# Four edits to a tuned encoder layer: a scale moved forward, a split between two prompt products, weight loads cut into eight pieces, and the down projection begun with another product

## The chip, the core and the metric

The kernel runs on one core of one Trainium2 chip. The time is device microseconds (us) of one execution on that core; the median of three executions is what counts. Five instruction queues run beside each other and wait for one another by semaphores: TensorE (PE, with its weight loads listed apart as PEld), VectorE (DVE), ScalarE (ACT), GpSimd (POOL), and SyncE (SP), which here only issues DMAs.

## The reference, cut to what matters

```python
h = _rmsnorm(x, g_mix)
z = h @ w_in
# qa, ka, va, qb, kb, vb and gates are slices of z
o_a, _ = _banded_attention(qa, ka, va, A_WINDOW, 1, rel_bias[:, :A_HEADS], sink)
o_b = _dilated_mixture(qb, kb, vb, rel_bias[:, A_HEADS:])
merged = gates[:, :, 0] * (o_a.reshape(b, S, A_Q) @ w_branch_a) + gates[:, :, 1] * (o_b @ w_branch_b)
x = x + merged @ w_out
h = _rmsnorm(x, g_mlp)
return x + jnp.square(jax.nn.relu(h @ w_up)) @ w_down
```

One layer of this is run, with a last RMSNorm behind it, over 1024 "sample" rows and 256 "prompt" rows of width 1024; the hidden width is 4096. Everything is float32.

## The kernel before, in words

A float32 product is made of three products of rounded parts. Each operand is split into a high part (ACT copies it rounded, the name ends in `hi`) and a low part (DVE subtracts the high one, the name ends in `lo`), and `six` multiplies low by high, high by low and high by high. For the sample rows the seven products of a Strassen-Winograd scheme (A11, A12, S2, S3, S1, A22, S4) stand for eight: sums and differences of weight quarters (`ta`, `tb`) and of activation quarters are split and multiplied. The prompt rows go through plain products (`prompt`). Every engine's queue runs in the order in which the program is written; there is no planner. Generators (`turns`, `b`/`nb`, `hooks`, `side`) are advanced at written places to put one stage's instructions among another's.

The stages in order are these. RMSNorm of ten tiles of 128 rows: `square(t)` and `scale(t)` on ACT and DVE, then `turn` transposes the tile on PE (names `tr`), beside the first value products (L794, `v`). Then pairs of 128-column blocks of `w_in`: `pair` runs the seven products of one pair while `right_pair` loads, combines and splits the weights of the next (`raw`, `ta`, `tb`, `whi`, `wlo`). The last five pairs are "late": between their products attention B runs, a step at each `beside()`; each step needs its `qk` and `v` loads, which SP issues (L509, L512, L524). Then attention A, the branch products and `w_out`. Then sixteen calls `up(j)` for the up projection: seven sample products and two prompt products each, with the split of the next weights between them, squared ReLU on ACT and DVE (L1869 to L1874), and on POOL four combinations of the result (L1945 to L1948) that are stored to `scr_u` by seven DMAs. `up(0)` has its two prompt products at its end, and the first two products of `up(1)` are computed before them.

The down projection is 28 jobs `(n, g)`: product n of seven, for the eight hidden blocks of group g. The first fourteen jobs take groups 0 and 1, two jobs to a product, and accumulate in the same PSUM banks. A job is 60 matmuls of 128x512 (`dn`). While job s runs, `ahead(s)` issues the `fetch` of the left side of job s+2 from `scr_u` (`uraw`, three DMAs), weight blocks (`loads`) and residual rows (`residual`, five DMAs to `v`), splits the weights of job s+1 (`dhi`, `dlo`; from a loaded block, or from a difference `t` of two that POOL makes in `combine`, L1698), and splits the left side of job s+1 (`uhi`, `ulo`, `up`; `left`, three parts, each after one of the job's five tiles). After a pair of jobs DVE adds each tile to the residual sums (L1852). `begin` does the same for job 0 and part of job 1 during the last `up`, one step at each hook.

`up(15)` is the last of these calls. The instructions of interest are, by the names of the profile: `xn<-xt,rs,gm` and `tr<-ident,xn` in the first stage, `raw<-in_w_in_dram` and `qk<-scr_qb` in the late pairs, `whi<-ta`, `wlo<-ta`, `wlo<-tb` in `up(0)` and `up(1)`, and `dhi`, `ulo`, `t` and `v<-scr_x` around the first jobs of the down projection.

Of the kernel before, what the change touches and what calls it, by code (L numbers as in the profile page):

```python
# [10 lines left out]
F32 = mybir.dt.float32  # L11
# [4 lines left out]
P = 128  # L16
# [81 lines left out]
def encoder_kernel(  # L98
# [224 lines left out]
    def steps_of(gen, n):  # L323
        for _ in range(n):
            next(gen, None)
# [43 lines left out]

    def right_pair(cols, out, make=wslot, vector=False):  # L370

# [4 lines left out]
        for i in range(2):  # L376
            nc.sync.dma_start(raw[i], cols[i])
        yield

# [289 lines left out]
    with ExitStack() as pre:  # L669
# [173 lines left out]
        scale(2)  # L843
        next(turns[0], None)
        pss = [bank("mm", "v") for _ in range(2)]
        for t, i in ((0, 0), (0, 1), (1, 0), (1, 1), (0, 2), (1, 2), (0, 3), (1, 3)):
# [3 lines left out]
        next(turns[2])  # L850
        square(3)
        next(turns[1], None)
        scale(3)
        square(4)
# [53 lines left out]
    if True:  # L908
# [104 lines left out]
        def pair(b, parts, cols, nxt, hooks, beside, late):  # L1013
# [5 lines left out]
            np_ = []  # L1019
            nb = right_pair([w_in3[:, :, c : c + P] for c in nxt], np_, wslot, late) if nxt else iter(())  # L1020

# [5 lines left out]
            def behind():  # L1027
                beside()
                if not late:
                    steps_of(b, 2)  # L1030

            one.begin()
# [10 lines left out]
            next(hooks, None)  # L1043
            one.direct(NS, NP, pa)
            beside()
            seven(x, S2, parts[1], 0, False, False, beside)
            c2 = stage("c", n=2)
            nc.scalar.activation(c2, x, AF.Copy, scale=one.scale)
            behind()
            if late:  # L1050
                next(nb, None)
            z = bank("mm", "z")
            seven(z, S3, parts[1], 1, last=False, mid=beside)
            c7 = stage("c", n=2)
            nc.scalar.activation(c7, z, AF.Copy, scale=two.scale)
            two.begin()
            beside()
            next(hooks, None)
            seven(x, S1, parts[2], 0, False, False, beside)
            two.sum(512, 512, x, c7)  # L1060
            beside()
            if not late:
                steps_of(nb, 3)
# [592 lines left out]
    TO = ((C22, C12), (C11,), (C12,), (C21, C22), (C12,), (C21,), (C11,))  # L1656
    JOBS = [(n, 2 * p + i) for p in range(NG // 2) for n in range(7) for i in range(2)]

    class Down:
# [6 lines left out]

        def block(self, g, k, h, make=wslot, queue=None):

            b = self.blocks[g, k, h] = [make("raw", (P, 2, 512)) for _ in range(2)]
            for i in range(2):  # L1670
                j = 4 * g + 2 * i
                (queue or nc.sync).dma_start(b[i], w_down4[:, j : j + 2, k, 512 * h : 512 * h + 512])

        def loads(self, n, g):
            if n == 1:
                self.block(g, 1, 1, slot)
            elif n == 4:
                self.block(g, 1, 0, slot)
            elif n == 5 and g < NG - 2:
                self.block(g + 2, 0, 0)  # L1680
                self.block(g + 2, 0, 1)

# [70 lines left out]
        def begin(self):  # L1753

            self.block(0, 0, 0, wslot, nc.scalar)
            self.block(0, 0, 1, slot, nc.scalar)
            self.fetch(*JOBS[0])
            yield
            self.combine(*JOBS[0])
            yield  # L1760
            yield
            self.block(1, 0, 0)
            self.block(1, 0, 1)
            yield
            self.right(*JOBS[0], slot)
            self.combine(*JOBS[1])
            yield
            self.left(*JOBS[0], 0)
            self.left(*JOBS[0], 1)
            yield  # L1770
            self.fetch(*JOBS[1])
            yield
            self.left(*JOBS[0], 2)

        def ahead(self, s):
# [86 lines left out]
    with ExitStack() as pre:  # L1862
# [22 lines left out]

        begun = {}

        def up(j, b, parts, hooks):
# [6 lines left out]

            u = [stage(f"u{i}", TH) for i in range(7)]
            u11, u12, u22, u21 = u[A11], u[A12], u[A22], u[S3]
            start = begin(parts)
# [4 lines left out]
            steps_of(b, 2)  # L1903
            next(hooks, None)
            x, y, c1 = begun[j] if j in begun else next(start)
            relu2_sum(u11[:, :512], y, c1)
# [40 lines left out]
            nc.gpsimd.tensor_tensor(u[S3], u11, u21, op=ALU.subtract)  # L1947
            nc.gpsimd.tensor_tensor(u[S4], u12, u[S2], op=ALU.subtract)  # L1948
            for i in (A11, S1, A22, S2, S3, A12, S4):
                nc.sync.dma_start(scr_u[j // 4][:, i, j % 4, :], u[i])  # L1950
            next(hooks, None)
# [48 lines left out]
```

## Time and profile before

| | |
|---|---|
| median of 3 runs | 1686.62 us (1685.78 to 1687.19) |
| profiled execution, its own time | 1685.92 us |
| its span | 1684.1 us, granted clock 0.999 |
| PE busy | 1667.8 us (99%) |
| DVE, ACT, POOL busy | 952.2, 718.3, 511.6 us |
| DMA | 260.35 MB, mean 155 GB/s |

A row of a timeline begins with the start in us from the span's beginning and the length in us; the bracket at its end is the time for which the engine stood idle before it, and what ended that. Matmuls overlap in the pipeline: two that follow each other without a gap start 0.23 us apart though each is shown 0.39 us long. A row with xN stands for N instructions in a row. A row of the waits gives engine, line, what was waited for, total us, times, longest us. A row of windows gives, for a stretch, its length, the busy time of each engine and at its end granted clock, DMA share and GB/s.

### The profile page before, as it was taken

The numbers are of one execution on the slowest core, as the hardware profiler recorded it, in microseconds if no ns is written. First come the engines' busy times: TensorE is split into PE (matmuls) and PEld (weight loads), VectorE is DVE, ScalarE is ACT, GpSimd is POOL, SyncE is SP. The second block draws the span as 40 slices with busy tenths as digits, with TensorE's granted clock in tenths as the row PEclk, the third lists the DMA queues.
The fourth block names the chain that finished last, engine by engine and source line by source line (L and its number), as shares of the span: only waits on it lengthen the run. The fifth ranks groups of instructions, "written<-read, shape, count | busy, mean of one in ns | idle before, by whom it ended". The sixth has DMA issues, their size and how long they took to land.

```text
span 1684.1 us, 24915 instructions
## 1 busy us (share of the span) xinstructions
PE 1667.8 (99%) x9268; PEld 1413.9 (84%) x9268; DVE 952.2 (57%) x1544; ACT 718.3 (43%) x1485; POOL 511.6 (30%) x404
## 2 busy tenths in 40 slices
PE   8999999999999999999999999999999999999998
PEld 7898888887788888888888888888888888888886
DVE  6732233455563565677278445545457767666575
ACT  6332323346663556654175333333334333333345
POOL 1312222122111463200100646556456322314150
PEclk9999999999999999999999999999999999999999
DMA  7416552677676793845121443443346845533333
GB/s 247 150 58 127 134 129 77 163 193 196 191 198 189 202 244 118 293 130 198 38 88 58 160 152 111 136 160 119 121 160 241 293 155 166 207 101 114 119 119 125
DMA packets 224408, 260.35 MB, mean 155 GB/s; under 512 B 29568, under 2 KB 154288, under 8 KB 224288
## 3 DMA queue, kind: packets, MB, share of 16 engines
q1 hardware_dynamic: 214976, 235.60, 44.1%
q0 software_dynamic: 7936, 20.54, 5.5%
q10 hardware_dynamic: 1376, 2.62, 0.4%
q8 instruction: 73, 1.20, 0.3%
q14 instruction: 47, 0.39, 0.1%
HBM read 173.03 MB, written 90.92 MB: 157 GB/s over the span
## 4 chain that ended last, share of the span: by engine, by line
PE 92%; DVE 3%; ACT 2%; DMA 1%; issue 1%; SPq 1%; POOL 0%; DVEq 0%; ACTq 0%
PE dn L347 20%; PE x L347 19%; PE mm L192 14%; PE z L347 9%; PE v L794 5%; PE mm L347 5%; PE y L347 5%; PE sc L347 3%; PE pv L347 3%; PE pv L1173 1%; PE pt L1157 1%; PE sc L537 1%; PE pv L582 1%; PE pt L569 1%; PE sc L1131 1%
## 5 line engine op out<-in xcount | busy, mean ns | idle before, releaser
L347 PE MATMUL dn<-dhi,ulo 128*128 128x512 f32 x448 | 174.5, 390 | 2.0 <-DVE ulo L186 2.0
L347 PE MATMUL dn<-dlo,uhi 128*128 128x512 f32 x448 | 174.3, 389 | 0.0
L347 PE MATMUL dn<-dhi,uhi 128*128 128x512 f32 x448 | 174.3, 389 | 0.0
L347 PE MATMUL x<-chi,wlo 128*128 128x512 f32 x424 | 167.2, 394 | 1.7 <-DVE wlo L314 1.6
L347 PE MATMUL x<-clo,whi 128*128 128x512 f32 x424 | 165.7, 391 | 0.1
L347 PE MATMUL x<-chi,whi 128*128 128x512 f32 x424 | 165.1, 389 | 0.0
L314 DVE TENSOR_TENSOR wlo<-ta,whi 128x1024 fp32r<-128x1024 f32 x30 | 55.7, 1857 | 178.5 <-ACT whi L312 178.5
L314 DVE TENSOR_TENSOR wlo<-raw,whi 128x1024 fp32r<-128x1024 f32 x60 | 90.4, 1506 | 97.8 <-ACT whi L312 97.8
L389 POOL TENSOR_TENSOR tb<-raw 128x512 f32<-128x512 f32 x25 | 32.8, 1312 | 364.4 <-DMA raw<-in_w_in_dram 147.0
L347 PEld LDWEIGHTS dn<-dhi,ulo 128*128 128x128 f32 x448 | 84.1, 188 | 20.3 <-DVE ulo L186 2.8
L186 DVE TENSOR_TENSOR ulo<-uraw,uhi 128x1024 fp32r<-128x1024 f32 x56 | 92.4, 1669 | 11.6 <-ACT uhi L185 11.6
L347 PEld LDWEIGHTS dn<-dhi,uhi 128*128 128x128 f32 x448 | 84.1, 188 | 17.4
L347 PEld LDWEIGHTS dn<-dlo,uhi 128*128 128x128 f32 x448 | 84.1, 188 | 17.3
L347 PEld LDWEIGHTS x<-chi,wlo 128*128 128x128 f32 x424 | 79.8, 188 | 17.8 <-DVE wlo L314 1.3
L347 PEld LDWEIGHTS x<-chi,whi 128*128 128x128 f32 x424 | 79.6, 188 | 17.0
L347 PEld LDWEIGHTS x<-clo,whi 128*128 128x128 f32 x424 | 79.8, 188 | 14.8 <-DVE clo L314 0.4
L1698 POOL TENSOR_TENSOR t<-raw,t 128x1024 f32<-128x1024 f32 x16 | 46.6, 2928 | 144.0 <-DMA raw<-in_w_down_dram 144.0
L1852 DVE TENSOR_TENSOR v<-v,dn 128x512 f32<-128x512 f32 x90 | 59.5, 681 | 39.7 <-PE dn L347 35.5
L1945 POOL TENSOR_TENSOR u<-u,u 128x640 f32<-128x640 f32 x16 | 25.6, 1597 | 159.3 <-ACT u L1870 159.3
L347 PE MATMUL dn<-dhi,up 128*128 128x512 f32 x224 | 73.5, 389 | 0.0
L347 PE MATMUL z<-chi,wlo 128*128 128x512 f32 x184 | 72.0, 391 | 0.0
L347 PE MATMUL z<-chi,whi 128*128 128x512 f32 x184 | 71.6, 389 | 0.0
(325 smaller groups left out, 4619.9 us busy)
## 6 DMA issues: line engine op xcount, KB each, us to landing
scr_u<-u SPq DMA_DIRECT2D x112, 320.0 KB, 2.6
uraw<-scr_u SPq DMA_DIRECT2D x56, 512.0 KB, 4.5
raw<-in_w_in_dram SPq DMA_DIRECT2D x33, 512.0 KB, 5.7
raw<-in_w_up_dram SPq DMA_DIRECT2D x32, 512.0 KB, 5.4
raw<-in_w_down_dram SPq DMA_DIRECT2D x28, 512.0 KB, 6.8
sg<-scr_g SPq DMA_DIRECT2D x32, 256.0 KB, 6.4
uraw<-scr_u SPq DMA_DIRECT2D x28, 256.0 KB, 4.5
v<-scr_v SPq DMA_DIRECT2D x96, 64.0 KB, 2.7
```

What stands on the lines that cost most here:

```text
L186: nc.vector.tensor_tensor(lo, src, hi.bitcast(F32), op=ALU.subtract)
L192: nc.tensor.matmul(ps, a, b, start=i == 0, stop=i == len(seq) - 1)
L314: nc.vector.tensor_tensor(lo, src, hi.bitcast(F32), op=ALU.subtract)
L347: nc.tensor.matmul(ps, a, b, start=first and i == 0, stop=last and i == len(seq) - 1, skip_group_check=True)
L389: (nc.vector if vector else nc.gpsimd).tensor_tensor(o, x, y, op=ALU.subtract)
L537: nc.tensor.matmul(at(k, h)[p0 : p0 + nq, :], qk[rows, p0 : p0 + nq], qk[rows, P + P * a : P + P * a + W], start=True, stop=True, skip_gro ...
L569: nc.tensor.transpose(ps[:, P * a : P * a + P], s[:, h, P * k : P * k + P], ident)
L582: nc.tensor.matmul(pv[HALVES[h], c + p0 : c + p0 + nq], v[:, a + k, HALVES[h]], pt[:, 2 * k + h, p0 : p0 + nq], start=k == 0, stop=k == W ...
L794: nc.tensor.matmul(ps[:, :n], a, b, start=k == 0 and j == 0, stop=k == KC - 1 and j == 2)
L1698: nc.gpsimd.tensor_tensor(o, a, b, op=ALU.subtract)
L1852: nc.vector.tensor_tensor(v, v, ps, op=ALU.add)
L1945: nc.gpsimd.tensor_tensor(u[S1], u21, u22, op=ALU.add)
```

## The change

Four edits stand in one diff.

First, in the opening stage `square(3)` and `scale(3)` are written ahead of the value products of tiles 0 and 1, rather than behind them. Second, at the end of `up(0)` two more steps of the next weights' split are taken between the two prompt products. Third, the weights of a late pair are loaded by eight DMAs of 128 KB instead of two of 512 KB, and these are issued one at a time at eight places of the pair's program (`piece`). Fourth, the first fourteen down jobs begin with product 6 (its left side is A12, its weight a loaded block that needs no `combine`), so that the order of products is 6, 0, 1, 2, 3, 4, 5; block (0,1,0) is loaded in `up(14)` to a pool of its own, the others in `up(15)` and in job 0 on SP (no load is issued from ACT any more); the loads of a group's second pass are issued at n = 4; the residual loads go one in each of the first four jobs; and the seven stores of an `up` are issued by the next `up`, behind its first hook. `store_u` is new, and `begin` is rewritten.

```diff
-    def right_pair(cols, out, make=wslot, vector=False):
+    def right_pair(cols, out, make=wslot, vector=False, step=KC):
         raw = [make("raw", (P, KC, P)) for _ in range(2)]
         for i in range(2):
-            nc.sync.dma_start(raw[i], cols[i])
-        yield
+            for c in range(0, KC, step):
+                nc.sync.dma_start(raw[i][:, c : c + step, :], cols[i][:, c : c + step, :])
+                if step < KC:
+                    yield
+        if step == KC:
+            yield
...
         next(turns[0], None)
+        square(3)
+        scale(3)
         pss = [bank("mm", "v") for _ in range(2)]
...
         next(turns[2])
-        square(3)
         next(turns[1], None)
-        scale(3)
         square(4)
...
-            nb = right_pair([w_in3[:, :, c : c + P] for c in nxt], np_, wslot, late) if nxt else iter(())
+            nb = right_pair([w_in3[:, :, c : c + P] for c in nxt], np_, wslot, late, 2 if late else KC) if nxt else iter(())
...
+            def piece_beside():
+                beside()
+                piece()
...
+            piece()
             beside()
-            seven(x, S2, parts[1], 0, False, False, beside)
+            seven(x, S2, parts[1], 0, False, False, piece_beside)
...
-            if late:
-                next(nb, None)
+            piece()
             z = bank("mm", "z")
-            seven(z, S3, parts[1], 1, last=False, mid=beside)
+            seven(z, S3, parts[1], 1, last=False, mid=piece_beside)
...
+            piece()
             next(hooks, None)
-            seven(x, S1, parts[2], 0, False, False, beside)
+            seven(x, S1, parts[2], 0, False, False, piece_beside)
             two.sum(512, 512, x, c7)
             beside()
-            if not late:
+            if late:
+                steps_of(nb, 2)
+            else:
                 steps_of(nb, 3)
...
-    JOBS = [(n, 2 * p + i) for p in range(NG // 2) for n in range(7) for i in range(2)]
+    JOBS = [(n, 2 * p + i) for p in range(NG // 2) for n in (range(7) if p else (6, *range(6))) for i in range(2)]
...
         def loads(self, n, g):
-            if n == 1:
+            if n == 6 and g == 0:
+                self.block(1, 0, 0)
+                self.block(1, 0, 1)
+            elif n == 1:
                 self.block(g, 1, 1, slot)
             elif n == 4:
                 self.block(g, 1, 0, slot)
-            elif n == 5 and g < NG - 2:
-                self.block(g + 2, 0, 0)
-                self.block(g + 2, 0, 1)
+                if g < NG - 2:
+                    self.block(g + 2, 0, 0)
+                    self.block(g + 2, 0, 1)
...
         def begin(self):
-            self.block(0, 0, 0, wslot, nc.scalar)
-            self.block(0, 0, 1, slot, nc.scalar)
             self.fetch(*JOBS[0])
             yield
-            self.combine(*JOBS[0])
-            yield
-            yield
-            self.block(1, 0, 0)
-            self.block(1, 0, 1)
+            self.block(1, 1, 0)
             yield
             self.right(*JOBS[0], slot)
-            self.combine(*JOBS[1])
+            yield
+            self.fetch(*JOBS[1])
             yield
             self.left(*JOBS[0], 0)
             self.left(*JOBS[0], 1)
-            yield
-            self.fetch(*JOBS[1])
+            self.block(0, 0, 0)
+            self.block(0, 0, 1)
             yield
             self.left(*JOBS[0], 2)
...
-            if s in (0, 2, 4):
-                self.residual((C22, C11, C21)[s // 2])
-            if s == 0:
-                self.residual(C12)
+            if s < 4:
+                self.residual((C11, C22, C12, C21)[s])
...
             next(hooks, None)
+            store_u()
+            u = [stage(f"u{i}", TH) for i in range(7)]
...
                 prompt_out(prompt(parts[0]), (u11, u21))
+                steps_of(nb, 2)
             prompt_out(prompt(parts[3], "sc"), (u12, u22))
...
-            for i in (A11, S1, A22, S2, S3, A12, S4):
-                nc.sync.dma_start(scr_u[j // 4][:, i, j % 4, :], u[i])
+            stores_u.extend((scr_u[j // 4][:, i, j % 4, :], u[i]) for i in (A11, S1, A22, S2, S3, A12, S4))
...
+            if j == last - 1:
+                down.block(0, 1, 0, lambda name, shape: late.tile(list(shape), F32, name=name, tag="block", bufs=2))
             b = up(j, *b, entering() if not j else down.begin() if j == last else iter(()))
+        store_u()
```

PE's own order is the same before and after. What the edits move on the other queues is shown at three places. The lines of the changed kernel are shifted by a few: the ReLU rows L1869 and L1870 become L1880 and L1881, DVE's L1873, L1874 and L1852 become L1884, L1885 and L1863, SP's L509, L524 and L923 become L513, L528 and L927.

At the end of `up(0)`, ACT's queue before (`u<-sc` is the ReLU of the second prompt product, `c_9601` the copy of `up(1)`'s S2 product):

```order
L1870 ACTIVATE u_9272<-u_9272 128x128
L1869 ACTIVATE u_9270<-sc 128x128
L1870 ACTIVATE u_9270<-u_9270 128x128
L1869 ACTIVATE u_9274<-sc 128x128
L1870 ACTIVATE u_9274<-u_9274 128x128
L312 ACTIVATE whi<-ta 128x1024
L312 ACTIVATE whi<-tb 128x1024
L1917 ACTIVATE c_9601<-x 128x512
```

and with the change:

```order
L1881 ACTIVATE u_9321<-u_9321 128x128
L312 ACTIVATE whi<-ta 128x1024
L1880 ACTIVATE u_9319<-sc 128x128
L1881 ACTIVATE u_9319<-u_9319 128x128
L1880 ACTIVATE u_9323<-sc 128x128
L1881 ACTIVATE u_9323<-u_9323 128x128
L312 ACTIVATE whi<-tb 128x1024
L312 ACTIVATE whi<-raw 128x1024
```

The split of `ta` now stands ahead of the ReLU that waits for the second prompt product; on DVE `wlo<-tb` likewise comes ahead of the sum `u<-y` of `up(1)`.

In the first late pairs, SP's queue before:

```order
L923 DMA scr_g_130<-z 128x256
L524 DMA v<-scr_v 128x128 x2
L509 DMA qk<-scr_qb_121 128x128
L509 DMA qk<-scr_kb_127 128x128
...
L377 DMA raw<-in_w_in_dram 128x8x128 x2
L524 DMA v<-scr_v 128x128 x2
```

and with the change:

```order
L378 DMA raw<-in_w_in_dram 128x2x128
L927 DMA scr_g_130<-z 128x256
L528 DMA v<-scr_v 128x128 x2
L513 DMA qk<-scr_qb_121 128x128
L513 DMA qk<-scr_kb_127 128x128
...
L378 DMA raw<-in_w_in_dram 128x2x128 x2
L528 DMA v<-scr_v 128x128 x2
```

(each of the two has the pair of `qk` rows twice). Two more pieces follow the next step's `qk` loads, and three more those of the step after.

At the end of `up(15)` and in the first down jobs, DVE's queue before (`t_` are the differences that POOL makes, `v<-v,dn` the additions of results):

```order
L186 TENSOR_TENSOR ulo<-uraw,uhi 128x1024 x2
L186 TENSOR_TENSOR up<-uraw,up 128x512
L186 TENSOR_TENSOR dlo<-t_12511,dhi 128x1024
L186 TENSOR_TENSOR dlo<-t_12512,dhi 128x1024
L186 TENSOR_TENSOR ulo<-uraw,uhi 128x1024 x2
L186 TENSOR_TENSOR up<-uraw,up 128x512
L186 TENSOR_TENSOR dlo<-raw,dhi 128x1024 x2
L1852 TENSOR_TENSOR v<-v,dn 128x512 x2
L186 TENSOR_TENSOR ulo<-uraw,uhi 128x1024
```

and with the change:

```order
L186 TENSOR_TENSOR up<-uraw,up 128x512
L186 TENSOR_TENSOR dlo<-raw,dhi 128x1024 x2
L186 TENSOR_TENSOR ulo<-uraw,uhi 128x1024 x2
L186 TENSOR_TENSOR up<-uraw,up 128x512
L186 TENSOR_TENSOR dlo<-t_12663,dhi 128x1024
L186 TENSOR_TENSOR dlo<-t_12664,dhi 128x1024
L1863 TENSOR_TENSOR v<-v,dn 128x512
L186 TENSOR_TENSOR ulo<-uraw,uhi 128x1024
L1863 TENSOR_TENSOR v<-v,dn 128x512
L186 TENSOR_TENSOR ulo<-uraw,uhi 128x1024
```

The first two jobs split loaded blocks, and the differences are first needed for job 2. The two `ulo` of that job now stand behind one and two additions, which wait for `v` loads that SP issues behind four 512 KB weight loads.

More of the change, by code (lines that the diff above doesn't have):

```diff
@@ L1030, in behind, with piece @@
                     steps_of(b, 2)
+            def piece():
+                if late:
+                    next(nb, None)
+            def piece_beside():
+                beside()
+                piece()
             one.begin()
@@ L1057, in pair @@
             beside()
+            piece()
             next(hooks, None)
-            seven(x, S1, parts[2], 0, False, False, beside)
+            seven(x, S1, parts[2], 0, False, False, piece_beside)
             two.sum(512, 512, x, c7)
             beside()
-            if not late:
+            if late:
+                steps_of(nb, 2)
+            else:
                 steps_of(nb, 3)
@@ L1665, in make, with block @@
             return self.late.tile(list(shape), dt, name=name, tag="l4", bufs=8)
-        def block(self, g, k, h, make=wslot, queue=None):
+        def block(self, g, k, h, make=wslot):
             b = self.blocks[g, k, h] = [make("raw", (P, 2, 512)) for _ in range(2)]
@@ L1671, in block @@
                 j = 4 * g + 2 * i
-                (queue or nc.sync).dma_start(b[i], w_down4[:, j : j + 2, k, 512 * h : 512 * h + 512])
+                nc.sync.dma_start(b[i], w_down4[:, j : j + 2, k, 512 * h : 512 * h + 512])
         def loads(self, n, g):
-            if n == 1:
+            if n == 6 and g == 0:
+                self.block(1, 0, 0)
+                self.block(1, 0, 1)
+            elif n == 1:
                 self.block(g, 1, 1, slot)
@@ L1886, in encoder_kernel, with store_u @@
         begun = {}
+        stores_u = []
+        def store_u():
+            while stores_u:
+                nc.sync.dma_start(*stores_u.pop(0))
         def up(j, b, parts, hooks):
@@ L1894, in prompt_out @@
                     relu2(d[:, 512:], ps[:, P * i : P * i + P])
-            u = [stage(f"u{i}", TH) for i in range(7)]
-            u11, u12, u22, u21 = u[A11], u[A12], u[A22], u[S3]
             start = begin(parts)
@@ L1904, in up @@
             next(hooks, None)
+            store_u()
+            u = [stage(f"u{i}", TH) for i in range(7)]
+            u11, u12, u22, u21 = u[A11], u[A12], u[A22], u[S3]
             x, y, c1 = begun[j] if j in begun else next(start)
```

## The prediction

> **What bounds the kernel now.** I read the page's head first, then the waits of PE, then the timelines around each wait.
>
> ```profile
> span 1684.1 us, 24915 instructions
> PE 1667.8 (99%) x9268; PEld 1413.9 (84%) x9268; DVE 952.2 (57%) x1544; ACT 718.3 (43%) x1485; POOL 511.6 (30%) x404
> ```
>
> PE is busy for all but 16.3 us of the span, part of which lies ahead of its first instruction and behind its last. Its order and its work stay the same, so the change can win only idle time of PE, and can lose by making new idle time. The waits of PE say what there is:
>
> ```profile
> PE dn L347 <- DVE ulo L186: 2.0, 2, 1.2
> PE x L347 <- DVE wlo L314: 1.6, 2, 1.1
> PE tr L338 <- DVE tab L856: 1.1, 1, 1.1
> ```
>
> These 4.7 us are five waits. The edits act on four of them (one of the two `ulo` waits belongs to a later job); beside them a wait costs a little more than its idle time, since the matmul that follows starts the pipeline anew (0.50 us long instead of 0.39).
>
> **First edit, the scale of the fourth tile.**
>
> ```profile
> 24.73 0.39 PE L794 MATMUL v<-vhi,hlo 128*128 128x512 f32 x1
> 26.21 1.07 PE L338 MATMUL tr<-ident,xn 128*128 128x128 f32 x8 [1.10 <-DVE tab L856]
> ...
> 21.98 1.21 ACT L765 ACTIVATE hhi<-tr 128x256 fp32r<-128x256 f32 x4 [4.30 <-PE tr L338]
> 25.25 0.40 ACT L779 ACTIVATE a<-tr 128x256 f32<-128x256 f32 x1
> ...
> 24.78 1.28 DVE L739 SCALAR_TENSOR_TENSOR xn<-xt,rs,gm 128x1024 f32<-128x1024 f32 x1
> 30.21 1.28 DVE L739 SCALAR_TENSOR_TENSOR xn<-xt,rs,gm 128x1024 f32<-128x1024 f32 x1
> ...
> 32.59 1.03 PE L338 MATMUL tr<-ident,xn 128*128 128x128 f32 x8
> ```
>
> The transposes of tile 3 wait for `xn`, which DVE ends at 26.06 (24.78 + 1.28). The name `tab` in the bracket is only the next DVE instruction. The change puts the square, the root and the scale ahead of `hhi`, ahead of which ACT stands idle for 4.30 us; they need 1.08 to 1.11 us and 0.29 us on ACT and 1.28 us on DVE, so `xn` is ready some 5 us earlier. What comes next is the end of the four copies L778/L779, which free the banks: 25.65 before, and 1.3 us earlier without the square among them, so 24.3. PE can go at 24.73 + 0.23 = 24.96. Gain 26.21 - 24.96 = 1.25 us. Bounds: 0, if tile 4 takes the wait over, and 1.25. Tile 4's transposes start at 32.59 with `xn` ready at 31.49 (30.21 + 1.28), a slack of 1.10 us; with PE 1.25 earlier and ACT's chain moved up as well, it stays positive. I take 1.25.
>
> **Second edit, the split between the prompt products.**
>
> ```profile
> 924.99 0.28 ACT L1869 ACTIVATE u<-sc 128x128 f32<-128x128 f32 x1 [1.75 <-PE sc L347]
> 926.02 1.04 ACT L312 ACTIVATE whi<-ta 128x1024 fp32r<-128x1024 f32 x1
> ...
> 927.10 1.75 DVE L314 TENSOR_TENSOR wlo<-ta,whi 128x1024 fp32r<-128x1024 f32 x1 [4.76 <-ACT whi L312]
> 931.83 0.69 DVE L1873 TENSOR_TENSOR u<-y,c 128x512 f32<-128x512 f32 x1 [2.98 <-POOL u L1947]
> 933.79 1.21 DVE L314 TENSOR_TENSOR wlo<-tb,whi 128x1024 fp32r<-128x1024 f32 x1
> ...
> 927.55 0.28 PE L347 MATMUL pv<-phi,whi 128*128 128x256 f32 x1
> 928.90 0.50 PE L347 MATMUL x<-chi,wlo 128*128 128x512 f32 x1 [1.08 <-DVE wlo L314]
> 934.27 0.39 PE L347 MATMUL z<-chi,whi 128*128 128x512 f32 x1
> 935.15 0.47 PE L347 MATMUL x<-chi,wlo 128*128 128x512 f32 x1 [0.49 <-DVE wlo L314]
> ```
>
> PE waits twice in `up(1)`. `whi<-ta` stands behind the ReLU that waits for the second prompt product. Moved ahead of it, it goes into ACT's idle 1.75 us and ends by about 924.3; `wlo<-ta`, at 1.2 to 1.75 us, is done by 926.1, where PE wants it at 928.90 - 1.08 = 927.82. `wlo<-tb` now stands ahead of `u<-y`, which waits for POOL until 931.83; it can run from 928, 5 us before PE's second need at 934.66 (935.15 - 0.49). What is queued behind them: the ReLU rows, four of 0.26 to 0.31 us, start at the same 925 since they wait for PE. `u<-y` keeps its place behind POOL. Idle time that goes: 1.08 + 0.49 = 1.57 us; with the two restarts and the bits of idle in the pipeline that the matmul starts show (928.90 is 1.35 us after the last prompt matmul's start at 927.55, where 0.12 is the pace, so 1.23; 935.15 is 0.88 after the last, where 0.23 is the pace, so 0.65) at most 1.23 + 0.65 and another 0.2 in the next four matmuls. Gain 1.57 to 2.08, taken 1.95.
>
> **Third edit, eight pieces.**
>
> ```profile
> 354.00:515.00 161.00, 160.89 (x1315) 128.44 (x1315) 95.06 (x385) 95.22 (x320) 31.68 (x56) 1.00 0.68 191
> ...
> 402.92 4.08 SPq L524 DMA_DIRECT2D v<-scr_v  x4
> ...
> raw<-in_w_in_dram SPq DMA_DIRECT2D x8, 512.0 KB, 5.8
> ```
>
> In the late pairs PE stands idle for 0.11 us in 161 us. That is all this edit can win, with a restart 0.27 us; I take 0.2, because SP is held less. (Four `v` loads took 4.08 us behind the two of 512 KB.) What it costs: six more issues in each of four pairs, at the 0.4 to 0.5 us at which that queue's issues follow each other (qk on it: 0.38 and 0.42), 24 x 0.45 = 10.8 us of SP, three pieces in a row at the worst place, 1.35 us ahead of the next `qk` loads. It is nothing as long as these loads have the time; that is the second rival.
>
> **Fourth edit, down begun with A12.**
>
> ```profile
> 1294.07 0.40 PE L347 MATMUL dn<-dhi,ulo 128*128 128x512 f32 x1
> 1296.85 0.50 PE L347 MATMUL dn<-dhi,ulo 128*128 128x512 f32 x1 [1.23 <-DVE ulo L186]
> 1309.23 0.39 PE L347 MATMUL dn<-dhi,ulo 128*128 128x512 f32 x1
> 1322.83 0.39 PE L347 MATMUL dn<-dhi,ulo 128*128 128x512 f32 x1
> ...
> 1292.64 6.40 POOL L1698 TENSOR_TENSOR t<-raw 128x1024 f32<-128x1024 f32 x2 [4.46 <-DMA raw<-in_w_down_dram]
> ...
> 1292.24 4.56 DVE L186 TENSOR_TENSOR ulo<-uraw,uhi 128x1024 fp32r<-128x1024 f32 x2
> 1296.72 2.87 DVE L186 TENSOR_TENSOR up<-uraw,up 128x512 fp32r<-128x512 f32 x1
> 1319.41 0.69 DVE L1852 TENSOR_TENSOR v<-v,dn 128x512 f32<-128x512 f32 x1 [2.73 <-DMA v<-scr_x]
> 1320.02 1.22 DVE L186 TENSOR_TENSOR ulo<-uraw,uhi 128x1024 fp32r<-128x1024 f32 x1
> ...
> 1301.06 7.85 SPq L1950 DMA_DIRECT2D scr_u<-u  x6
> 1309.00 0.94 SPq L1718 DMA_DIRECT2D uraw<-scr_u  x2
> ...
> 1309.00:1323.00 14.00, 14.00 (x63) 11.62 (x62) 7.88 (x10) 6.53 (x7) 0.00 (x0) 1.00 0.99 346
> ```
>
> Job 0 lasts from 1294.07 to 1309.23, 15.16 us, job 1 the 13.60 us of an undisturbed job. The loss of 1.56 us is the wait for the second `ulo`: beside POOL's differences `t` the two take 4.56 us, beside an idle POOL one takes 1.22. With A12 first, POOL makes no difference ahead of job 0, ACT and DVE split loaded blocks, and the two `ulo` stand ahead of the sum `u<-z`; I put them at 1291, 3 us before the need. Gain 1.56, bounds 1.23 (the idle time alone) and 1.56. The copy of product S3 now follows two `dhi` of about 1 us on ACT; it may hold PE for up to 0.5 us. I take nothing for it.
>
> What is late next is job 2. Its start would be 1294.07 + 2 x 13.60 = 1321.27. Its left side is fetched when SP is through with the stores that here end at 1309, by then at about 1305, since POOL starts the combinations of `u` without the differences ahead. Behind this fetch stand four weight loads of 512 KB and then the five `v`. At the stretch's 346 GB/s the 1.25 MB of the fetch and 2 MB of blocks take 3.8 + 6.1 us, so the first `v` lands between 1316 and 1318.5 (before: its addition at 1319.41 had waited for such a load). Then DVE needs 0.69 + 1.22 us for the first `ulo` and as much for the second, wanted 1.36 us into the job (six matmuls): ready at 1320 to 1322.4, wanted by 1322.63. That leaves nothing to 0.2 us with POOL quiet; but POOL makes the differences of job 3 in those very microseconds. With 2.3 us (half of 4.56) for each `ulo` the second ends 2.2 us later. Between 0 and 1.9 us I take 0.5, nearer to the undisturbed row, because the weight loads for POOL's work land before the `v` loads and POOL then is partly through. Jobs 3 and later have a whole job's time more. Net gain 1.56 - 0.5 = 1.06; bounds -0.7 and 1.56.
>
> The Trainium skill, page "SBUF — State Buffer", section "Who interferes with whom", says that a VectorE instruction with both inputs in SBUF contends with a GpSimd instruction that reads SBUF, and that the loser of the shared port waits for the winner's whole instruction. The trace agrees: `up` of 0.68 us alone took 2.87 us and ended at 1299.59, 0.55 us after POOL's 6.40 us ended at 1299.04. By this rule a `ulo` in job 2 waits for the end of POOL's instruction, and the sum would be that of the first rival.
>
> **The sum.** 1.25 + 1.95 + 0.2 + 1.06 = 4.46 us. Against the profiled execution's own 1685.92 us that is 1681.5. That execution lies 0.7 us under the median of the runs, 1686.62; against the median the forecast is 1682.1 us.
>
> **The rivals.**
>
> *Job 2 takes the wait over.* POOL's two differences of 3.2 us (6.40 for two) fall on both `ulo`: the first ends at POOL's end, 1.0 us late, and the second 0.5 to 0.9 more. Then the fourth edit gives 1.56 - 1.7 and the whole 3.3 us: 1683.3, on the edge of what can be measured. For it speaks the `ulo` row beside POOL, against it that the `v` loads gate both. Chance 0.2.
>
> *The pieces hold back the attention's loads; slower.* If SP's extra issues in the late pairs reach PE in full, they cost 10.8 us, and the time is 1686.6 - 4.26 + 10.8 = 1693.2. It decides when 7.6 of the 10.8 us reach PE (4.26 to be made good, and 3.37 for the bound). For it: SP issues without a break in part of this stage, and PE was seen to idle there. Against it: SP waits elsewhere in the same pair, and loses the hold of 2.2 us (4.08 less the some 1.9 us of four plain issues) behind the large loads. Chance 0.07.
>
> *The waits move but stay.* The first and second edit only hand the wait on, to tile 4 and to the `whi<-raw` of `up(1)`, and the gain is that of job 0 alone, 1.2 us net: 1685.4. Against it stand the slacks of 1.1 us and 5 us. Chance 0.08.
>
> **How the numbers follow.** Forecast 0.65, the rivals 0.2, 0.07 and 0.08. A change of 0.2%, 3.4 us, is what a measurement can tell, so under 1683.25 is faster. The forecast's own range is 1680.5 (all terms at their better end, 1.25 + 2.08 + 0.27 + 1.56 = 5.16, less the 0.84 by which the lowest run was under the median, rounded down) to 1683.2 (1.57 and 0.4 in the second and fourth term). Up to 1685 it takes in the first rival and most of the third. Faster: 0.63 of the forecast and 0.1 of the first rival, 0.73. Slower: 0.06, nearly all of the second rival. Same: the rest, 0.21.
>
> **What would show it.** Right: PE's waits on `tab` and on `wlo` are gone from its list, the transposes of tile 3 start 0.23 us after the matmul ahead of them, and the first down job lasts 13.6 us. Wrong: a gap of PE 1 to 2 us long at the start of the third down job ahead of a `dn<-dhi,ulo`, with a `ulo` of over 2 us beside a POOL `t`; gaps ahead of `sc<-qk` between 354 and 515 us, after rows of three `raw` on SP; or a gap in `up(15)` ahead of the A22 product, behind the late copy of S3. What would make the forecast wrong altogether is a wait that no row of before shows, above all in job 2 to job 4, where each hangs on loads in a queue that moves 346 GB/s at a DMA share of 0.99.

## The result, and the profile after

The changed kernel takes 1682.48 us (median of twelve executions, 1680.55 to 1686.18) where the kernel before took 1687.04 us (twelve executions beside it): a ratio of 0.9974 with a 95% interval of 0.9965 to 0.9983, that is 4.6 us or 0.26% faster. The forecast was 1682.1 us and 4.5 us.

The head of the page of the changed kernel, and its list of what PE waited for (engine, line, what was waited for, us in total, times, longest):

```profile
span 1678.9 us, 24941 instructions
PE 1666.4 (99%) x9268; PEld 1413.8 (84%) x9268; DVE 953.1 (57%) x1544; ACT 718.3 (43%) x1485; POOL 509.5 (30%) x404
```

```profile
PE tr L338 <- DVE xn L743: 1.7, 2, 0.9
PE warm L711 <- POOL ident masks.py:199: 1.4, 1, 1.4
PE dn L347 <- DVE ulo L186: 0.7, 1, 0.7
PE sc L1146 <- DVE m L1148: 0.7, 1, 0.7
PE v L798 <- DVE vlo L705: 0.7, 1, 0.7
```

The waits on `tab` (1.1 us) and on `wlo` (1.6 us) are gone, and of the 2.0 us on `ulo` one wait of 0.7 us is left, the one near 1603 us that the change does not touch. Since PE runs the same 9268 matmuls in the same order in both kernels, the starts of equal matmuls can be subtracted. That difference, read from the start of the program to its end, grows in steps, and each step has a place:

| place in the kernel before, us | step, us |
|---|---|
| 26.2, transposes of tile 3 | -1.24 |
| 452 to 457, `sc<-qk` | -0.38 |
| 540, `mm` | -0.16 |
| 614, `pt<-ident,s` of attention A | -0.70 |
| 929 and 935, products of `up(1)` | -1.38 and -0.77 |
| 1297, job 0 of down | -1.54 |
| 1322 to 1325, end of job 1 and start of job 2 | +0.59 |
| last matmul | -5.58 in all |

The span is 5.28 us shorter, 0.3 us less than the last matmul is earlier: between the landing of the last transfer and the end of the span stand 1.23 us after and 0.98 us before. This belongs to the fourth edit: the trace of the kernel with that edit undone (below) has 0.97 us there, and all ten traces of kernels with it have 1.21 to 1.23 us. What in the edit makes it is not shown.

The places themselves, in the timelines of the changed kernel (start, length, instruction, idle time before it). The fourth tile: DVE makes its `xn` from 19.36 and PE's transposes start 1.24 us earlier.

```profile
19.36 1.29 DVE L743 SCALAR_TENSOR_TENSOR xn<-xt,rs,gm 128x1024 f32<-128x1024 f32 x1
...
24.98 1.04 PE L338 MATMUL tr<-ident,xn 128*128 128x128 f32 x8
```

The split in `up(0)`: `whi<-ta` now runs ahead of the ReLU `u<-sc`, both `wlo` follow at once, and only `u<-y` still waits for POOL.

```profile
920.62 1.04 ACT L312 ACTIVATE whi<-ta 128x1024 fp32r<-128x1024 f32 x1
922.47 0.28 ACT L1880 ACTIVATE u<-sc 128x128 f32<-128x128 f32 x1 [0.81 <-PE sc L347]
...
921.69 1.22 DVE L314 TENSOR_TENSOR wlo<-ta,whi 128x1024 fp32r<-128x1024 f32 x1 [1.86 <-ACT whi L312]
924.57 1.76 DVE L314 TENSOR_TENSOR wlo<-tb,whi 128x1024 fp32r<-128x1024 f32 x1 [1.66 <-ACT whi L312]
929.32 0.69 DVE L1884 TENSOR_TENSOR u<-y,c 128x512 f32<-128x512 f32 x1 [2.98 <-POOL u L1965]
```

The start of the down projection: job 0 starts at 1289.40, job 1 at 1303.03 (13.63 us later), job 2 at 1316.81 (13.78 later), with a second small wait at its seventh matmul, 1318.49.

```profile
1289.40 0.40 PE L347 MATMUL dn<-dhi,ulo 128*128 128x512 f32 x1
...
1303.03 0.39 PE L347 MATMUL dn<-dhi,ulo 128*128 128x512 f32 x1
...
1316.81 0.47 PE L347 MATMUL dn<-dhi,ulo 128*128 128x512 f32 x1
...
1318.49 0.50 PE L347 MATMUL dn<-dhi,ulo 128*128 128x512 f32 x1
...
1312.83 0.69 DVE L1863 TENSOR_TENSOR v<-v,dn 128x512 f32<-128x512 f32 x1 [4.44 <-DMA v<-scr_x]
1313.44 3.27 DVE L186 TENSOR_TENSOR ulo<-uraw,uhi 128x1024 fp32r<-128x1024 f32 x1
1316.63 0.68 DVE L1863 TENSOR_TENSOR v<-v,dn 128x512 f32<-128x512 f32 x1
1317.22 1.21 DVE L186 TENSOR_TENSOR ulo<-uraw,uhi 128x1024 fp32r<-128x1024 f32 x1
...
1310.87 4.76 POOL L1716 TENSOR_TENSOR t<-raw 128x1024 f32<-128x1024 f32 x2 [4.83 <-DMA raw<-in_w_down_dram]
```

DVE waits 4.44 us for the first residual `v`, and the `ulo` behind it takes 3.27 us beside POOL's differences, which end at 1315.63; the `ulo` ends 1.08 us after that, at 1316.71. Job 2 starts 0.1 us behind it.

### The profile page after: what moved, and what is told of

Same layout as the page of the kernel before. It is cut to its first block, busy times and chain, and to the rows that moved or that the text cites. A ratio compares the mean times of both kernels' runs of the same rounds, so it can differ in the third digit from the quotient of the medians.

```text
span 1678.9 us, 24941 instructions
## 1 busy us (share of the span) xinstructions
PE 1666.4 (99%) x9268; PEld 1413.8 (84%) x9268; DVE 953.1 (57%) x1544; ACT 718.3 (43%) x1485; POOL 509.5 (30%) x404
## 5 line engine op out<-in xcount | busy, mean ns | idle before, releaser
L1863 DVE TENSOR_TENSOR v<-v,dn 128x512 f32<-128x512 f32 x90 | 59.2, 680 | 34.3 <-PE dn L347 29.8
L186 DVE TENSOR_TENSOR dlo<-raw,dhi 128x1024 fp32r<-128x1024 f32 x32 | 47.3, 1500 | 45.3 <-ACT dhi L185 44.4
```

Of the source, the lines that this page charges most:

```text
L186: nc.vector.tensor_tensor(lo, src, hi.bitcast(F32), op=ALU.subtract)
L1863: nc.vector.tensor_tensor(v, v, ps, op=ALU.add)
```

## The experiments

Each is measured against the kernel before, on the same chip; the medians of the kernel before were 1686.80, 1686.75 and 1686.82 us in the three sessions. The first four undo one of the edits in the changed kernel. The changed kernel's 1682.48 us, to which their medians are set, stood beside a kernel before of 1687.04 us in a session of its own, and the intervals of their four ratios overlap that of the changed kernel (0.9965 to 0.9983). So what one edit is worth is read from the traces, and the difference of two medians only supports it.

### The first edit undone

```diff
-        square(3)
-        scale(3)
         pss = [bank("mm", "v") for _ in range(2)]
...
         next(turns[2])
+        square(3)
         next(turns[1], None)
+        scale(3)
```

> The changed kernel with the first edit alone undone (square and scale of the fourth tile behind the value products again). Theory, each edit is worth its own wait: the transposes of tile 3 wait again for about 1.1 us on `xn`, PE's order of events is 1.24 us later from there to the end, and nothing else changes; time about 1.2 us above the changed kernel, 3.3 us under the kernel before. Rival, the waits are linked, and the shift of 1.24 us is taken up by a later wait (of attention A near 614 us, 0.7 us in the two traces): the end moves by 0.5 us or by 1.9 us instead.

1683.68 us (9 executions; ratio 0.9981, 0.9971 to 0.9991), 1.2 us above the changed kernel. Its waits of PE:

```profile
PE sc L1146 <- DVE m L1148: 2.0, 2, 1.3
...
PE tr L338 <- DVE tab L860: 1.1, 1, 1.1
```

The wait on `tab` is back and PE is 1.26 us later from there on. The traced execution was also held 1.7 us more in attention A (near 630 us) and about 1 us elsewhere. The median over nine executions, 1.2 us above, speaks for the edit's own wait of 1.26 us as its price; that the wait in attention A has nothing to do with the edit is not shown by one trace.

### The second edit undone

```diff
                 prompt_out(prompt(parts[0]), (u11, u21))
-                steps_of(nb, 2)
             prompt_out(prompt(parts[3], "sc"), (u12, u22))
```

> The changed kernel with the second edit alone undone (no two split steps between the prompt products of up(0)). Theory: both waits of PE for `wlo` in up(1) come back, 1.08 and 0.49 us of idle time, 2.15 us by the starts of matmuls, and the time is 2.1 us above the changed kernel, 2.4 us under the kernel before. Rival, only the first wait hung on the ReLU and the second on the POOL work of up(0), which the other edits leave: about 1.4 us above the changed kernel.

1684.26 us (11 executions; 0.9982, 0.9973 to 0.9991), 1.8 us above the changed kernel.

```profile
PE x L347 <- DVE wlo L314: 1.6, 2, 1.1
```

Both waits are back, and the steps by matmul starts are 1.34 us at the first and 0.77 us at the second, 2.1 us together.

### The third edit undone

`right_pair` and `pair` are those of the kernel before, all else as changed:

```diff
-            for c in range(0, KC, step):
-                nc.sync.dma_start(raw[i][:, c : c + step, :], cols[i][:, c : c + step, :])
-                if step < KC:
-                    yield
-        if step == KC:
-            yield
+            nc.sync.dma_start(raw[i], cols[i])
+        yield
```

> The changed kernel with the third edit alone undone (two loads of 512 KB for a late pair, in one place). Theory: PE's waits for `qk` near 452 and 457 us come back, 0.13 and 0.25 us, and the time is 0.4 us above the changed kernel, which these rounds may not tell from none; the trace does. Rival: the pieces also lie behind the 0.16 us near 540 us and the 0.70 us near 614 us that went between the two traces, and the time is 1.2 us above the changed kernel, with a wait `pt <- ACT s` near 614 us in its trace.

1682.46 us (7 executions; 0.9967, 0.9956 to 0.9978): the changed kernel's time. Its trace has one wait for `qk` of 0.5 us, and three small ones in attention A.

```profile
PE sc L537 <- DMA qk<-scr_kb: 0.5, 1, 0.5
...
PE pt L1157 <- ACT s L1143: 0.7, 3, 0.3
```

Neither theory is borne out: the edit is worth nothing that these executions can tell, where 0.4 and 1.2 us were expected. The wait of `pt` for `s` that the rival named is there, but the repetition below, which has the pieces, has one of 0.3 us too. It also shows why a single trace misled.

### The fourth edit undone

`JOBS`, `block`, `loads`, `begin`, `ahead` and the stores of `up` are those of the kernel before:

```diff
-    JOBS = [(n, 2 * p + i) for p in range(NG // 2) for n in (range(7) if p else (6, *range(6))) for i in range(2)]
+    JOBS = [(n, 2 * p + i) for p in range(NG // 2) for n in range(7) for i in range(2)]
...
-            stores_u.extend((scr_u[j // 4][:, i, j % 4, :], u[i]) for i in (A11, S1, A22, S2, S3, A12, S4))
+            for i in (A11, S1, A22, S2, S3, A12, S4):
+                nc.sync.dma_start(scr_u[j // 4][:, i, j % 4, :], u[i])
```

> The changed kernel with the fourth edit alone undone (down begun with product 0 again, its loads, residuals and the stores of each up at their former places). Theory: job 0 of the down projection lasts 15.1 us again, jobs 1 and 2 last 13.6 us each, and the time is 0.95 us above the changed kernel. Rival, the net of the fourth edit is nothing or a loss, since the two traces show 1.5 us won in job 0 and 0.6 us lost in jobs 1 and 2, and 0.3 us at the very end: the time is within 0.5 us of the changed kernel.

1683.68 us (10 executions; 0.9981, 0.9972 to 0.9990), 1.2 us above the changed kernel.

```profile
PE dn L347 <- DVE ulo L186: 1.9, 2, 1.2
```

By matmul starts job 0 loses 1.49 us and jobs 1 and 2 win back 0.6 us, and the end of the span wins back the 0.3 us of above. That leaves 0.6 us, between the theory's 0.95 us and the 0.5 us at which the rival began; the times can't tell the two apart.

### The residual loads first

```diff
-            self.loads(n, g)
             if s < 4:
                 self.residual((C11, C22, C12, C21)[s])
+            self.loads(n, g)
```

> The changed kernel with, in down job 0, the five residual loads issued ahead of the four 512 KB weight loads instead of behind them. In the changed kernel the first residual lands at 1312.8 us and the first `ulo` of job 2 then runs 3.27 us beside POOL's differences. Theory, the wait in job 2 is that collision: the residuals land some 4 us earlier, both `ulo` run at 1.2 us ahead of POOL's work, which starts later, and jobs 1 and 2 last 13.6 us each; 0.6 us under the changed kernel. Rival, the fetch of job 2's left side and not the residual holds DVE, or POOL's later differences now hit the `ulo` of job 3: jobs 1 to 3 keep a stall of 0.5 us or more, and the time is the changed kernel's.

```profile
1309.34 0.68 DVE L1863 TENSOR_TENSOR v<-v,dn 128x512 f32<-128x512 f32 x1
1309.93 1.22 DVE L186 TENSOR_TENSOR ulo<-uraw,uhi 128x1024 fp32r<-128x1024 f32 x1
1311.07 0.68 DVE L1863 TENSOR_TENSOR v<-v,dn 128x512 f32<-128x512 f32 x1
1311.67 1.22 DVE L186 TENSOR_TENSOR ulo<-uraw,uhi 128x1024 fp32r<-128x1024 f32 x1
...
1315.24 4.75 POOL L1716 TENSOR_TENSOR t<-raw 128x1024 f32<-128x1024 f32 x2 [8.17 <-PE dn L347]
```

DVE no longer waits for the residual; both `ulo` are done 2.3 us before POOL begins, and jobs 1 and 2 last 13.60 us each. The steps from job 1 to job 2 sum to -0.6 us against the changed kernel. The time, 1681.99 us (8 executions; 0.9974, 0.9964 to 0.9984), lies 0.5 us under the changed kernel's, which these executions can't tell from none; the trace can.

### POOL without the two differences

```diff
             if n == 0:
                 self.t[g] = [slot("t1", (P, 2, 512)) for _ in range(2)]
+                if g == 1:
+                    for o in self.t[g]:
+                        nc.gpsimd.memset(o, 0.0)
+                    return
```

> The changed kernel, but POOL fills job 3's weight differences with zeros instead of subtracting two blocks (so the first product of group 1 is left out of the result; the loads stay). Theory, a DVE instruction with two inputs in SBUF is held by a POOL instruction that reads SBUF: a POOL that only writes holds nothing, the first `ulo` of job 2 takes 1.2 us although the residuals still land as late, and job 2 lasts 13.6 to 13.7 us. Rival, the residual loads are what is late: `ulo` waits as before and jobs 1 and 2 together last 27.5 us or more, against 27.2 us undisturbed.

```profile
1314.21 0.69 DVE L1867 TENSOR_TENSOR v<-v,dn 128x512 f32<-128x512 f32 x1 [4.48 <-DMA v<-scr_x]
1314.82 1.22 DVE L186 TENSOR_TENSOR ulo<-uraw,uhi 128x1024 fp32r<-128x1024 f32 x1
...
1307.33 1.84 POOL L1708 MEMSET t<- 128x1024 f32 x2
```

This is one execution (1681.34 us), of a kernel that leaves the first product of group 1 out of its result. It parts the two causes. The residual lands as late as in the changed kernel (DVE waits 4.48 us for it, 4.44 there), yet the `ulo` takes 1.22 us instead of 3.27 and jobs 1 and 2 last 13.60 us. So what holds job 2 in the changed kernel is POOL beside `ulo`, not the late residual alone. The zeros need no load, so POOL wrote them at 1307.33 and was through before the `ulo`; that a writing POOL beside a `ulo` holds nothing is therefore not shown by it.

### Eight pieces in one place

```diff
             for c in range(0, KC, step):
                 nc.sync.dma_start(raw[i][:, c : c + step, :], cols[i][:, c : c + step, :])
-                if step < KC:
-                    yield
-        if step == KC:
-            yield
+        yield
```

(`pair` is that of the kernel before, so the eight stand where the two stood.)

> The changed kernel with the eight 128 KB pieces of a late pair issued one behind the other at the place of the former two loads. It parts the size of the loads from their spread. Theory, spreading is what matters and it matters little: eight issues in a row hold SP for some 3.6 us in one place, the following `qk` loads come that much later, PE waits 0.5 to 2 us for `qk` in each pair, 3 us in all, and the time is 1 to 4 us above the changed kernel. Rival, the size alone matters: the time is the changed kernel's within 0.5 us.

1684.89 us (10 executions; 0.9992, 0.9982 to 1.0001), 2.4 us above the changed kernel.

```profile
400.96 4.82 SPq L378 DMA_DIRECT2D raw<-in_w_in_dram  x8
...
411.39 1.36 PE L538 MATMUL sc<-qk 64*128 64x256 f32 x8 [1.28 <-DMA qk<-scr_kb]
```

The eight hold SP for 4.82 us, and two of the pairs then lose 1.28 and 1.16 us of PE at the `qk` loads behind them. So small pieces in one place are worse than two large loads; spread over the pair, they cost nothing that can be told.

### Sixteen pieces

```diff
-            nb = right_pair([w_in3[:, :, c : c + P] for c in nxt], np_, wslot, late, 2 if late else KC) if nxt else iter(())
+            nb = right_pair([w_in3[:, :, c : c + P] for c in nxt], np_, wslot, late, 1 if late else KC) if nxt else iter(())
...
-                if step < KC:
+                if step < KC and c % 2:
                     yield
```

> The changed kernel with sixteen pieces of 64 KB, two at each of the eight places: 32 more issues on SP in the four late pairs. Theory, SP has the room, and a late load shows on PE only where a step had under 0.5 us in hand: PE idles up to 1 us more between 350 and 515 us and the time is 0 to 1 us above the changed kernel. Rival, the issues of SP reach PE in full: 32 x 0.45 = 14.4 us above the changed kernel, or a good part of that.

1692.55 us (5 executions; 1.0033, 1.0019 to 1.0047): slower than the kernel before, 10 us above the changed one. The theory, 0 to 1 us, falls, and the rival, a good part of 14.4 us, holds. SP's row of six loads in a row, PE's wait, and four stretches of the timeline around the first large one (length, busy time of PE, PEld, DVE, ACT, POOL, granted clock, DMA share, GB/s):

```profile
366.82 2.83 SPq L378 DMA_DIRECT2D raw<-in_w_in_dram  x6
```

```profile
PE sc L541 <- DMA qk<-scr_kb: 7.6, 6, 2.3
```

```profile
370.00:374.00 4.00, 4.00 (x32) 3.40 (x30) 3.93 (x16) 2.19 (x10) 0.57 (x1) 1.00 0.99 310
374.00:378.00 4.00, 1.28 (x9) 0.66 (x8) 0.30 (x1) 0.33 (x1) 0.00 (x0) 1.00 0.80 225
378.00:382.00 4.00, 4.00 (x25) 3.59 (x24) 3.17 (x13) 2.67 (x10) 0.56 (x1) 0.57 0.60 183
382.00:386.00 4.00, 4.00 (x32) 2.91 (x31) 0.97 (x3) 0.44 (x2) 0.00 (x0) 1.00 0.55 150
```

PE idles 7.6 us for `qk` in three of the four pairs. The loads behind the six are issued 3.28 us later than in the changed kernel (the first row below is of this kernel, the second of the changed one), while the median time of a `qk` load from issue to landing, between 354 and 515 us, differs by 0.4 us at most (2.6 against 2.5 us for `scr_qb`, 3.0 against 2.6 us for the larger `scr_kb`). So it is mainly the place in SP's queue that makes them late, not the size of the pieces.

```profile
371.34 0.32 SPq L513 DMA_DIRECT2D qk<-scr_qb  x1
```

```profile
368.06 0.38 SPq L513 DMA_DIRECT2D qk<-scr_qb  x1
```

The rest of the loss is the clock. In each of the three pairs two waits stand close to each other, and during the second or just behind it a stretch begins in which the granted clock is 0.50:

```profile
378.28:381.69 3.41, 3.41 (x21) 3.08 (x18) 2.73 (x13) 2.36 (x9) 0.56 (x1) 0.50 0.60 191
429.48:436.30 6.82, 6.42 (x42) 5.79 (x43) 3.54 (x14) 2.13 (x9) 0.56 (x1) 0.50 0.72 203
480.68:484.09 3.41, 3.41 (x25) 3.08 (x22) 1.68 (x12) 1.54 (x7) 1.09 (x3) 0.50 0.80 225
```

Half of these 13.64 us is 6.8 us. With the 7.6 us of waits this makes 14.4 of the 14.8 us by which the last matmul is later than in the first trace of the changed kernel. (The traced execution, 1695.46 us, is the slowest of the five.)

### A version that is faster than both

The residuals first, and for job 24 (product 5, group 2) the load and POOL's differences a job earlier, ahead of the five multiplications `v<-v,gf`. It aims at the 0.9 us that every trace so far lost at job 23 (counted from 0), where in the changed kernel two `ulo` run from 1600.28 for 4.55 us beside these differences.

```diff
-            elif n == 4:
+            elif n == (3 if g == NG - 2 else 4):
                 self.block(g, 1, 0, slot)
...
-            if two:
+            three = JOBS[s + 3] if s + 3 < len(JOBS) else None
+            early = lambda job: job == (5, NG - 2)
+            if two and not early(two):
                 self.combine(*two)
+            if three and early(three):
+                self.combine(*three)
```

> The kernel with the residuals first (as in the run before), and for the second pass of the down projection: the differences of POOL for job 24 (product 5, group 2) made a job earlier, ahead of the five multiplications by the final norm's weights, and the load that they need a job earlier too. In all traces so far PE loses 0.9 us at job 23, where two `ulo` take 4.6 us beside these differences. Theory: the differences leave that place, both `ulo` of job 23 run at 1.2 us, the loss of 0.9 us goes; 1.5 us under the changed kernel, about 1681.0 us. Rival, POOL's work only moves on, to the `ulo` of job 22 or behind the multiplications, and some other job loses as much: 0.6 us under the changed kernel or nothing.

1681.33 us (5 executions, 1679.49 to 1681.78; 0.9962, 0.9948 to 0.9976), 5.5 us under the kernel before and 1.5 us under the changed kernel beside it (next run). The intervals of these two ratios overlap, so the gain over the changed kernel rests on the matmul starts below.

```profile
1567.32 3.37 POOL L1716 TENSOR_TENSOR t<-raw,t 128x1024 f32<-128x1024 f32 x1
...
1597.95 2.35 DVE L186 TENSOR_TENSOR ulo<-uraw,uhi 128x1024 fp32r<-128x1024 f32 x2
...
1602.74 0.39 PE L347 MATMUL dn<-dhi,ulo 128*128 128x512 f32 x1
```

The two `ulo` take 2.35 us together and job 23 starts without a gap. By matmul starts that place gives 1.0 us and job 2 gives 0.6 us. All 28 down jobs but the first (13.63) now last 13.60 us. The second `ulo` of jobs 22 and 24 still has 2.2 us or more in hand, so POOL's work did not only move on.

### The changed kernel once more

No edit.

> The changed kernel once more, beside the kernel of the run before on the same chip. Theory, its time is 1682.5 us as first measured, 4.6 us under the kernel before, and of its waits the ones near 10, 574 and 1603 us come back while those between 350 and 700 us fall elsewhere, since they hang on how DMAs land in one execution. Rival, its first trace with hardly a wait in that stage is what the kernel always does, and the trace agrees with the first within 0.2 us up to 900 us.

1682.81 us (7 executions; 0.9969, 0.9958 to 0.9980). In this trace PE waits in the late pairs, where the first trace had no wait at all:

```profile
PE sc L541 <- DMA qk<-scr_kb: 1.2, 1, 1.2
...
PE mm L192 <- ACT z L999: 0.6, 1, 0.6
```

The last matmul is 3.0 us later than in the first trace, all of it between 420 and 622 us. So this stage differs from one execution to the next by more than the third edit was expected to give, and the rival, that the first trace is what the kernel always does there, falls.

## Why the prediction was right

**The first edit, 1.25 us.** Right: 1.24 us by matmul starts, 1.2 us when undone. The copies that free the banks end at 24.31 us, where the working put them (24.3), and PE, no longer held, goes on at its own pace, at 24.98 against 24.96. Tile 4 kept its slack. The third rival, waits that move but stay, did not occur: nothing behind took the 1.24 us back.

**The second edit, 1.95 us.** Right, a little small in the trace (2.15 us) and a little large in the times (1.8 us when undone). Both waits went. The restart that the working added to the idle time of 1.57 us is real: the matmul starts give 1.38 and 0.77 us for idle times of 1.08 and 0.49.

**The third edit, 0.2 us.** The term is not borne out: without the edit the time is 1682.46 us, and 0.2 us is less than these medians can tell. The step that failed is that the 0.11 us of idle time of the one trace was taken as what the stage costs; with the same two large loads the trace of the third edit undone waited 0.5 us. In the traces of kernels with the pieces spread as here, PE's waits for `qk` are none in most, 0.6 us in one and 1.2 us in another. The second rival, SP's extra issues that hold back `qk`, was priced at 0.45 us an issue and ruled out for 24 issues; this was right for 24 and wrong for 56, where they come through. The margin was far smaller than its chance of 0.07 made it look: at double the number of pieces the kernel is slower than before by 5.8 us.

**The fourth edit, 1.06 us.** Right for the jobs: 0.95 us by matmul starts, of 1.54 won in job 0 and 0.59 lost in jobs 1 and 2, where the working had 1.56 and 0.5. What the working did not have is the 0.3 us that this edit costs at the end of the span, so some 0.65 us is left in the traces; the 1.2 us when undone is too rough to say otherwise. The cause it gave for the loss was the right pair, a residual behind weight loads and a `ulo` beside POOL, but it left open which; the run without POOL's differences shows that the collision makes the loss, and the run with the residuals first that an earlier residual avoids it. The first rival was this same collision with POOL's work on both `ulo` and 1.7 us; it fell on one. The sentence in which it was expected that POOL would be "partly through" by then is what happened: POOL began at 1310.87 and the `ulo` at 1313.44, into the second difference. The 0.5 us itself was a choice between 0 and 1.9 us, so that it came out so near is partly luck; the bound of nothing to 0.2 us with POOL quiet is borne out by the run without the differences, where jobs 1 and 2 lose nothing.

What the Trainium skill says of this port (page "SBUF — State Buffer", section "Who interferes with whom") agrees with these rows: the `ulo` ended 1.08 us after POOL did, about the length that it has alone. The prediction's step from this rule to the sum of the first rival did not follow, since only one of the two `ulo` met POOL.

**The sum.** 4.46 us were forecast and 4.56 us measured. That they agree to 0.1 us is partly luck: the interval of the ratio reaches from 2.9 to 5.9 us, and the repetition gave 4.0 us (1682.81 against 1686.82 us). In the traced executions the last matmul moved by 5.58 us, but 0.70 us at 614 us and 0.16 us near 540 us lie outside the change and come and go between executions of one kernel, as do the waits for `qk`. What the traces put down to the edits is 1.24 + 2.15 + 0.95 us, less 0.3 us at the end, some 4.0 us: the second term was too small by 0.2 us, which makes good in part what the third and the end took off. The four edits undone one at a time sum to 1.2 + 1.8 + 0.0 + 1.2 = 4.2 us; reckoned each from the kernel before of its own session, they sum to 5.1 us. So the times can't tell whether a part of the gain depends on two edits together.

## What to carry to other kernels

Where one engine is busy 99% of the span, list its waits one by one, find for each the instruction in whose queue it stood too far back, and move that one: by the matmul starts, each of the three moves here that had a wait to win won it to within 0.2 us of what was reckoned. What the move puts late elsewhere has to be taken off, here 0.6 us in jobs 1 and 2 and 0.3 us at the end of the span. A gain that rests on a tenth of a microsecond of idle time in one trace should be looked for in a second trace first. When loads are cut smaller, count the issues of the queue that makes them and the slack of what stands behind them: eight pieces spread out cost nothing that could be told, eight in one place 2.4 us, sixteen 10 us.

## What the runs showed of the hardware that was not expected

**A short wait can cost its length again through the clock.** With sixteen pieces PE idled 0.48 us and then 2.23 us with four small matmuls between them (busy 1.28 of four microseconds), and the granted clock of the next four microseconds was 0.57, 0.50 for 3.41 us of them; matmuls of 128x256 started 0.21 us apart instead of 0.12. After single waits of 1.28 us (eight pieces in one place) and 1.18 us (the changed kernel again) the clock stayed at 1.00. All in all 7.6 us of waits were followed by a loss of 6.8 us to the clock. The Trainium skill, page "TensorE: Matmul & The Clock Gate", section "Why this matters for your kernels", advises against idle gaps of over about 3 us; here no single gap was so long, and the clock fell behind a stretch of 3.4 us (374.03 to 377.45) in which PE did little.

**The loss grows in a jump.** 24 issues more on SP than before cost nothing that could be told, 56 more cost 10 us against the changed kernel. At the first wait the `qk` loads were issued 3.28 us later and PE waited 2.71 us, so the step had some 0.6 us in hand (an estimate from these two), and the clock then about doubled what was lost.
